# A row softmax on one core: TensorE in place of SyncE waits for the last stores

## The chip, the cores and the metric

The kernel runs on one core of a Trainium2 chip. A core has five engines, each with its own stream of instructions: TensorE (PE), VectorE (DVE), ScalarE (ACT), GpSimd (POOL) and SyncE (SP). They meet only through semaphores, counters that one instruction raises and another waits for. Transfers between the chip's main memory (HBM) and the core's working memory are made by 16 DMA engines; here SP alone issues them. The metric is the time of one execution on the device, in microseconds (us).

## The reference

A softmax over the last axis of a float32 array of 16 x 1024 x 512, that is over 16384 rows of 512 numbers:

```python
x_max = np.max(x, axis=-1, keepdims=True)
exp_x = np.exp(x - x_max)
return (exp_x / np.sum(exp_x, axis=-1, keepdims=True)).astype(np.float32)
```

33.55 MB are read and 33.55 MB written.

## The kernel before

**Tiles.** The 16384 rows are cut into 16 groups of 128 partitions x 8 rows (GROUPS, GROUP). The working memory holds a ring of 12 groups (RING), in which everything is done in place. Eight loads (L0 to L7) and eight stores (S0 to S7) of two groups each (LOADS, STORES) move 4096 KB apiece.

**Stages of a group.** DVE takes the negated maximum of each row (`rowmax`, line 145). ACT runs one loop over all groups (`exps`, lines 150 and 151, its work at line 134): per row an exponential with that maximum as its bias, which also leaves the row's sum. DVE inverts the sums (line 159), and DVE or POOL multiplies the group by them (line 161). Then SP stores it (line 131).

**What sets the order.** All is written out by hand. SEQUENCE is the order of DVE's and POOL's work: M and MM are maxima of one and of two groups, D a scaling on DVE, P one on POOL. ORDER is the order of SP's transfers after the first six loads: S0 S1 L6 L7 S2 S3 S4 S5 S6 S7. The loop at the end of the kernel goes through it; `store_scaled` (lines 169 to 171) waits until both groups of a store are scaled, and a load into a part of the ring that is used again waits for the store of what was there (line 197). The first six loads wait for nothing; `loads_at_the_head` puts the very first ahead of the start barrier. Two more barriers over all engines follow the first loads (they stand at line 179, `tc.close`); the profile shows their waits as EVENT_SEMAPHORE.

**The end.** `done_by` (lines 165 to 167) gives each store the semaphore that it raises by 16 when it has landed: `stored0` and `stored1` for S0 and S1, for which L6 and L7 wait, and one common semaphore, `others`, for S2 to S7 (number 120 in the trace). The last two lines of the kernel are the only place that waits for the stores S2 to S7:

```python
    nc.sync.wait_ge(others, 16 * (len(STORES) - 1 - max(awaited)))
    nc.sync.nop()
```

`awaited` is [0, 1], so the wait is for 16 * (8 - 1 - 1) = 96, six stores. The wait and the nop stand in the built program as one EVENT_SEMAPHORE instruction, the last of SP's stream (line 200 in the profile). TensorE does no work in this kernel; its stream has the barriers and nothing else.

Of the kernel before, what the change touches and what calls it, by code (L numbers as in the profile page):

```python
# [20 lines left out]
STORES = [2, 2, 2, 2, 2, 2, 2, 2]  # L21
# [39 lines left out]
def kernel(  # L61
# [5 lines left out]
    nc = tc.nc  # L67
# [15 lines left out]
    def sem(name):  # L83
        return ctx.enter_context(nc.semaphore(name))
# [18 lines left out]
    awaited = sorted(set(before.values()))  # L103
    stored = {k: sem(f"stored{k}") for k in awaited}
    others = sem("others")
# [19 lines left out]
    def load(k):  # L125
        g, n = LOAD_AT[k], LOADS[k]
        return nc.sync.dma_start(out=rows(g, n), in_=in_dram(x_rows, g, n))
# [62 lines left out]
    for transfer in ORDER.split():  # L190
# [3 lines left out]
        else:  # L194
# [1 line left out]
            since = max([a for a in awaited if a < last], default=-1)  # L196
            nc.sync.wait_ge(stored[last], 16 * (last - since))
            load(k).then_inc(loaded[k], 16)
    nc.sync.wait_ge(others, 16 * (len(STORES) - 1 - max(awaited)))
    nc.sync.nop()  # L200


# [28 lines left out]
```

## Time and profile before

| | |
|---|---|
| time, median of 3 runs | 159.92 us (159.79 to 159.99) |
| the profiled execution's own time | 160.08 us |
| its span, first to last instruction of the program | 158.8 us (158.764 in the trace) |
| DMA queue q1, share of 16 engines' span | 98.9%, 67.11 MB in 2304 packets |
| DVE, ACT, POOL busy | 121.8, 92.2, 42.3 us |
| last store issued by SP | 137.84 us after the span's start |
| wait on line 200 ends | 158.75 us after the span's start |

All times in the profile are counted from the span's start. The span holds only the program's own instructions; what the runtime executes ahead of them and after them lies outside. The page gives each engine's busy time, a strip of 40 equal slices of the span with the busy share of each in tenths, the DMA queues, and a chain that is followed back from the end. A "q" after an engine's name means its sequencer, which waits, branches and issues while the engine itself is idle. Beside instructions, the trace keeps the time of every update of every semaphore.

### The profile page before, as it was taken

How to read it: one execution, taken by the hardware profiler on the slowest of the kernel's cores; microseconds unless marked ns; L12 is line 12 of the kernel's file. 1: busy time of each engine (PE TensorE's matmuls, PEld its weight loads, DVE VectorE, ACT ScalarE, POOL GpSimd, SP SyncE). 2: the span in 40 equal slices, each digit the busy share in tenths (PEclk: the TensorE clock that was granted, in tenths of full speed). 3: DMA queues.
4: the chain of work that ended last, by engine and by line, in shares of the span. 5: the costliest groups of instructions: out<-in, count | busy, mean ns of one | idle time of the engine just before them, and what ended most of it. 6: DMA issues, size and time to landing. Idle time of an engine off the chain costs nothing.

```text
span 158.8 us, 572 instructions
## 1 busy us (share of the span) xinstructions
DVE 121.8 (77%) x36; ACT 92.2 (58%) x257; POOL 42.3 (27%) x10
## 2 busy tenths in 40 slices
DVE  0008979999999999999999499999999999700000
ACT  0300699969406999999988990899599300000000
POOL 0000000000007903930970790079049300000000
DMA  7999999999999999999999999999999999999996
GB/s 264 438 479 405 405 495 421 396 438 471 413 405 438 471 405 396 396 413 471 438 396 462 446 413 405 454 421 438 438 421 446 413 446 438 438 421 438 429 429 264
DMA packets 2304, 67.11 MB, mean 423 GB/s; under 512 B 256, under 2 KB 256, under 8 KB 256
## 3 DMA queue, kind: packets, MB, share of 16 engines
q1 hardware_dynamic: 2304, 67.11, 98.9%
HBM read 33.55 MB, written 33.55 MB: 423 GB/s over the span
## 4 chain that ended last, share of the span: by engine, by line
DMA 45%; DVE 39%; issue 2%; DVEq 0%
DMA ring<-in_x_dram 26%; DVE ring L161 22%; DMA out_dram<-ring 20%; DVE stat L145 16%; DVE recip L159 1%; DVEq L144 0%
## 5 line engine op out<-in xcount | busy, mean ns | idle before, releaser
L134 ACT ACTIVATE ring<-ring,stat x128 | 90.4, 707 | 28.1 <-ACTq L151 28.1
L145 DVE TENSOR_REDUCE stat<-ring 128x16 f32<-128x8192 f32 (+1 forms) x10 | 69.5, 6956 | 15.7 <-DMA ring<-in_x_dram 15.7
L161 POOL TENSOR_TENSOR ring<-ring,recip 128x4096 f32<-128x4096 f32 x6 | 42.1, 7016 | 81.8 <-DVE recip L159 81.8
L161 DVE TENSOR_TENSOR ring<-ring,recip 128x4096 f32<-128x4096 f32 x10 | 51.1, 5109 | 0.3
L134 ACT ACTIVATION_READ_ACCUMULATOR ring<-ring,stat x128 | 23.8, 186 | 0.0
L181 ACT ACT_TABLE_LOAD x1 | 1.3, 1283 | 4.0 <-PEq L179 4.0
L159 DVE RECIPROCAL recip<-stat 128x8 f32<-128x8 f32 x16 | 3.0, 190 | 0.0
L215 POOL MEMSET const-float32-0.0<- 128x1 f32 x1 | 0.1, 98 | 0.2 <-issue 0.2
L215 POOL MEMSET const-bfloat16-1.0<- 128x1 bf16 x1 | 0.1, 102 | 0.0
L215 POOL MEMSET const-uint8-127<- 128x1 uint8 x1 | 0.1, 102 | 0.0
L215 POOL MEMSET const-float32-1.0<- 128x1 f32 x1 | 0.1, 98 | 0.0
## 6 DMA issues: line engine op xcount, KB each, us to landing
ring<-in_x_dram SPq DMA_DIRECT2D x8, 4096.0 KB, 25.9
out_dram<-ring SPq DMA_DIRECT2D x8, 4096.0 KB, 24.0
```

Source lines behind the costliest of these rows:

```text
L134: return nc.scalar.activation(out=row, in_=row, func=EXP, bias=one, scale=1.0, accum_out=one)
L145: nc.vector.reduce_max(out=cols(stat, g, groups), in_=rows(g, groups), axis=AX, negate=True).then_inc(maxima, groups)
L159: nc.vector.reciprocal(out=cols(recip, g), in_=cols(stat, g)).then_inc(inverted, 1)
L161: engine.tensor_mul(out=rows(g), in0=rows(g), in1=spread(cols(recip, g))).then_inc(scaled[store_of(g)], 1)
L181: nc.scalar.preload_act_table(EXP)
L215: nc = _bacc.Bacc("TRN2", target_bir_lowering=False, num_devices=1)
```

## The change

The wait for `others` and the nop behind it are taken from SP's stream and put at the end of TensorE's. The condition, 96, is the same. Every other instruction keeps its engine and its place.

```diff
@@ -196,8 +196,8 @@
             since = max([a for a in awaited if a < last], default=-1)
             nc.sync.wait_ge(stored[last], 16 * (last - since))
             load(k).then_inc(loaded[k], 16)
-    nc.sync.wait_ge(others, 16 * (len(STORES) - 1 - max(awaited)))
-    nc.sync.nop()
+    nc.tensor.wait_ge(others, 16 * (len(STORES) - 1 - max(awaited)))
+    nc.tensor.nop()
```

## The prediction

> **What bounds the kernel now.** I read the page first, for the balance of engines and transfers.
>
> ```profile
> span 158.8 us, 572 instructions
> DVE 121.8 (77%) x36; ACT 92.2 (58%) x257; POOL 42.3 (27%) x10
> ...
> DVE  0008979999999999999999499999999999700000
> ...
> DMA  7999999999999999999999999999999999999996
> ...
> q1 hardware_dynamic: 2304, 67.11, 98.9%
> ...
> DMA 45%; DVE 39%; issue 2%; DVEq 0%
> ```
>
> The DMA row is full from end to end while the busiest engine is at 77%: the transfers set the time. PE has no row: it computes nothing. The chain's shares (DMA 45%, DVE 39%) follow one thread through work that lies under transfers, so I don't take DVE for the bound.
>
> Next SP's waits, the timeline of the end, and the table by stretches, whose last row starts where DVE is done (columns: stretch, its length, busy us of DVE, ACT, POOL, then PE clock, DMA share, GB/s).
>
> ```profile
> SPq L131 <- DVE ring L161: 112.0, 7, 36.0
> SPq L200 <- DMA out_dram<-ring: 20.6, 1, 20.6
> ```
>
> ```profile
> 133.38 4.42 DVE L161 TENSOR_TENSOR ring<-ring,recip 128x4096 f32<-128x4096 f32 x1
> 137.84 0.33 SPq L131 DMA_DIRECT2D out_dram<-ring  x1
> ```
>
> ```profile
> 138.00:159.00 21.00, 0.00 (x0) 0.00 (x0) 0.00 (x0) 1.00 0.92 396
> ```
>
> From 138.2 us on, nothing runs but the stores; SP waits 20.6 us for them on line 200, the wait that the change moves. Then the details of that line and of the barriers of line 179, the only place where PE and SP run the same instruction (ns, minimum/median/maximum; PEld is PE's own sequencer here).
>
> ```profile
> L200 SPq EVENT_SEMAPHORE  x1: 17/17/17, 158.7 to 158.7; - x1
> ```
>
> ```profile
> L179 SPq EVENT_SEMAPHORE  x2: 17/17/17, 3.6 to 3.9; - x2
> L179 ACTq EVENT_SEMAPHORE  x2: 17/17/17, 3.6 to 3.9; - x2
> L179 DVEq EVENT_SEMAPHORE  x2: 21/21/21, 3.6 to 3.9; - x2
> L179 PEldq EVENT_SEMAPHORE  x2: 51/51/51, 3.6 to 3.9; - x2
> ```
>
> One released wait costs PE 51 ns where SP, ACT and POOL need 17.
>
> **What lies after the span.** The profiled execution took 160.08 us, its span 158.764, so 1.32 us are outside. The trace keeps the time of every semaphore's updates, also of those that the program doesn't use. Semaphore 2 is such a one (the program has 96, 97 and 99 to 120), and it is updated nine times in each of several groups, us from the span's start:
>
> ```
> just before the program:  -0.375 -0.341 -0.302 -0.258 -0.235 | -0.123 -0.085 -0.051 -0.004
> closing, first group:      4.184 124.456 124.914 137.959 158.890 | 158.934 158.972 159.007 159.055
> closing, second group:    159.842 159.876 159.914 159.958 159.982 | 160.080 160.118 160.152 160.199
> ```
>
> Between the closing groups nearly all 256 semaphores are updated once, as in a reset: 207 to 255 at 159.015-159.102, 156 to 206 until 159.394, 105 to 155 until 159.422, 54 to 104 until 159.392, 3 to 53 until 159.617. I read this as a relay over the five engines, five steps up and four back, each waiting for the one before. The first closing group names them. At 4.184 us only PE has no work left, so **PE is first**. ACT's last instruction ends at 124.343 and POOL's at 124.386: steps two and three. DVE's ends at 137.808: step four. SP's wait ends at 158.764: step five, **SP is last**. So today everybody has handed on long before, and after the last landing the relay has only SP's step and the way back to do.
>
> **The change, part by part.** It adds no instruction: one wait with its nop, a single EVENT_SEMAPHORE in the trace, leaves SP and stands on PE. The order on each engine is otherwise the same; no DMA is moved, and SP issues all sixteen transfers as before (the last at 137.84). Behind the wait on PE stands only PE's relay step, and **all four other engines wait for that one**.
>
> 1. *Stores and compute: 0.* They don't know who waits. The last update of semaphore 120 (`others`) stays at 158.730.
> 2. *The last engine's arrival.* SP today: update at 158.730, wait starts 158.747 (+17 ns), lasts 17, relay step 126 ns later at 158.890; 160 ns in all. PE on the same road, from its own rows: in the barriers of line 179 PE starts 11 to 12 ns after SP on the same release (3.571 against 3.559, 3.898 against 3.887), so 28; the wait takes 51; from its last wait's end (3.898+0.051 = 3.949) to its relay step at 4.184 it took 235 ns, and from the last reset (159.617) to its next step (159.842) 225. That makes 28+51+235 = 314 ns. **Difference +0.154.** No row shows PE waiting for a DMA's semaphore with the relay behind it. The bounds for the road from the wait's end: 104 ns (ACT, from its last update at 124.352 to 124.456) and at least 528 (the step at 124.914 after POOL's end at 124.386; 571 if it is ACT's). By them the term goes from +0.023 to +0.447. I take 235, since it is PE's own, seen twice.
> 3. *The relay.* Today 158.890 to 159.055: 165 ns. With PE last to come, the whole relay runs after it. Whole relays with all engines waiting are shown: 357 ns (159.842 to 160.199) and 371 (-0.375 to -0.004). **Difference +0.192 to +0.206**, four hops up (34, 38, 44, 24 = 140) and a turn of 98 to 112 in place of 44. Bounds: 0, if the steps up don't depend on the order, and 0.206.
> 4. *Reset and second relay: 0 of their own.* They start from the first relay's end and move as a block. Already PE ends the resets last (159.617) and starts the second relay.
>
> SP's old road of 160 ns goes; it is hidden under the stores, and what is late next is PE's. The sum: 0.154 + 0.20 = **+0.35 us**, 160.43 against the profiled 160.08. That execution is 0.16 above the median of the runs shown (159.92); I carry the difference over: 159.92 + 0.35 = **160.27 us**.
>
> [...] The rows 51 and 17 for the same instruction don't look like equal sequencers, and I follow them. [...]
>
> **The rivals.**
>
> - *PE is no slower in this place* (waiting 155 us, it may have its next steps ready; 235 ns was just after a barrier), or the hops up are not serial. For it: no row shows this situation. Against: 225 ns again in another place, where PE had only resets behind it. Time: +0.20 (or +0.15 if only the relay is missing), 160.07 to 160.12.
> - *Not slower: arrivals are counted in any order, and the engine that comes last leaves first.* Then PE's late arrival (154 ns) is paid back where the way back, 165 ns today, no longer stands before PE's reset, the last to end. Price 0.154 - 0.165 = -0.01, 159.91; it decides as soon as the way back is worth more than PE's lateness. For it: the first closing group alone would look the same. Against: in the second group SP, free at 159.102, doesn't step until PE, free at 159.617, has; and the same gaps of 34, 38-39, 44, 23-24 come back. That is a fixed order.
> - *The time ends with the wait.* Then only the wait's own shift counts: 11 + 34 ns, +0.05, 159.97. Against: 1.32 us lie outside the span, and semaphore 2 goes on for 1.435 us after it, about as long. No view shows where the clock stops.
> - *PE leaves late*, as the step at 124.914 did: 528 in place of 235, +0.64, 160.56. For it: PE would not have run for 155 us. Against: its 235 and 225 agree.
>
> **How the numbers follow.** Forecast +0.35 (own range +0.30 to +0.40, 160.22 to 160.32): 0.72. PE not slower, or no serial hops: 0.12. Any order: 0.06. Ends with the wait: 0.04. Late exit: 0.06. About 0.2%, 0.32 us, is what a measurement of this kernel can tell from no change, and the forecast lies just over it: of its 0.72 I give 0.54 to slower by more and 0.18 to within. Slower: 0.54 + 0.06 = 0.60. Faster 0.02, the scatter of the second and third rival (the three runs lie 0.20 apart). The rest, 0.38, is within. The range goes from the third rival less some scatter, 159.95, to above the forecast with the scatter and half of the late exit, 160.45; it leaves out most of "any order" and of "late exit".
>
> **What would show it.** In the profile after: line 200 on PE with 51 ns, its start some 11 ns further from the last update of 120; SP's last record at 138.2; the span longer by about 0.05 only, since the relay lies outside. In semaphore 2: no updates between the program's start and 159 us, then PE's about 314 ns after the last landing, 34, 38, 44, 24 behind it, a turn near 100, and about 0.67 us from landing to the group's end in place of 0.325. The forecast is wrong in step 2 if that first number is nearer 160 ns, in step 3 if steps of other engines come before PE's, in step 1 if the last landing itself moves.

## The result, and the profile after

| | before | after |
|---|---|---|
| time, median of 7 runs each | 159.92 us (159.79 to 159.99) | 160.44 us (160.23 to 160.61) |
| ratio, 95% interval | | 1.003 [1.002, 1.004] |
| the profiled execution: time, span | 160.08, 158.764 us | 160.61, 158.994 us |
| last landing: the last raise of `others` (120) by a store, from the span's start | 158.730 us | 158.914 us |
| time of that execution less this landing | 1.350 us | 1.696 us |

Slower by 0.52 us, of the sign forecast; the sum had said +0.35. The measured 160.44 lies outside the forecast's own range (160.22 to 160.32) and only 0.01 us under the end of the whole range, 160.45. That end had been set for scatter and for half of a late exit of PE; the exit did not come, so that the time still lies inside is in part luck. The last row of the table holds the forecast sum: after the last store has landed, the changed kernel needs **0.346 us** more. The rest lies ahead of the landing and is taken up below.

The page of after; the lines answer to those shown of before:

```profile
span 159.0 us, 572 instructions
DVE 121.8 (77%) x36; ACT 92.3 (58%) x257; POOL 42.3 (27%) x10
...
DMA  7999999999999999999999999999999999999996
...
q1 hardware_dynamic: 2304, 67.11, 98.9%
...
DMA 45%; DVE 39%; issue 2%; DVEq 0%
```

Little in it tells of a change: 572 instructions again, busy times within 0.1 us, the same queue share and chain. The span alone is longer, by 0.230 us: 0.184 of it lies ahead of the landing, 0.046 is the wait's own shift (80 ns from the landing to the wait's end in place of 34). A page of the program's own span can't show a cost that is paid after it. SP's waits and the details of line 200 show what moved (ns, minimum/median/maximum, then first and last start in us):

```profile
SPq L131 <- DVE ring L161: 111.9, 7, 35.8
SPq L127 <- DMA out_dram<-ring: 18.9, 2, 9.5
```

```profile
L200 PEldq EVENT_SEMAPHORE  x1: 51/51/51, 158.9 to 158.9; - x1
```

SP's wait of 20.6 us is gone from its list; the same wait is now PE's, and lasts 51 ns after its release in place of 17. The rest is in semaphore 2 (us from the span's start):

```
closing, first group:     159.229 159.263 159.301 159.345 159.369 | 159.466 159.506 159.540 159.587
closing, second group:    160.378 160.412 160.450 160.494 160.518 | 160.616 160.654 160.689 160.735
```

Before, four of the five steps up stood at 4.184, 124.456, 124.914 and 137.959 us, long before the last landing. Now all nine come after it, PE's first, 315 ns behind the landing, and the whole first group runs 34, 38, 44, 24, 97, 40, 34 and 47 ns from step to step. It ends 673 ns after the landing; before it was 325.

### The profile page after: what moved, and what is told of

Same layout as the page of the kernel before. It is cut to its first block, busy times and chain, and to the rows that moved or that the text cites. A ratio compares the mean times of both kernels' runs of the same rounds, so it can differ in the third digit from the quotient of the medians.

```text
span 159.0 us, 572 instructions
## 1 busy us (share of the span) xinstructions
DVE 121.8 (77%) x36; ACT 92.3 (58%) x257; POOL 42.3 (27%) x10
## 4 chain that ended last, share of the span: by engine, by line
DMA 45%; DVE 39%; issue 2%; DVEq 0%
DMA ring<-in_x_dram 25%; DVE ring L161 22%; DMA out_dram<-ring 20%; DVE stat L145 16%; DVE recip L159 1%; DVEq L144 0%
## 5 line engine op out<-in xcount | busy, mean ns | idle before, releaser
L134 ACT ACTIVATION_READ_ACCUMULATOR ring<-ring,stat x128 | 24.4, 190 | 0.0
```

What stands on the lines that cost most here:

```text
L134: return nc.scalar.activation(out=row, in_=row, func=EXP, bias=one, scale=1.0, accum_out=one)
```

## The experiments

My theory: the five engines leave the program through a relay in the fixed order PE, ACT, POOL, DVE, SP and back; the engine that comes last pays its own road to its step (the time from the end of its wait to its update of semaphore 2), and all that stands behind its place runs after it. Rivals: only the last comer's road counts, not its place; an engine that stays inside the program, or an SP that is free under the stores, makes the transfers longer, which would be the missing 0.17 us. Since the landing scatters by some tenths from execution to execution (158.307 to 158.914 us), I read each run by what follows its own landing. All rows are from one profiled execution each:

| who waits for the stores | landing to that engine's step, ns | landing to the first group's end, ns | time less landing, us |
|---|---|---|---|
| SP (before; built anew) | 160; 160 | 325; 325 | 1.350; 1.352 |
| PE (after; second; third time) | 315; 314; 314 | 673; 672; 672 | 1.696; 1.697; 1.700 |
| SP and PE | 314 (PE's) | 672 | 1.694 |
| SP, PE until the last scaling | 160 | 322 | 1.349 |
| DVE | 193 | 435 | 1.456 |
| ACT | 157 | 480 | 1.503 |
| POOL | 578 | 864 | 1.888 |
| SP, and four more waits | 410 | 575 | 1.598 |
| PE, and four more waits | 742 | 1099 | 2.123 |

In all twelve profiles the last column is the one before it plus 1.021 to 1.028 us: what follows the first group costs the same whoever waits.

Time and span are also known for every single run, the span to 0.1 us, so the part outside the span can be averaged over all runs, without semaphore 2. The kernel before has 1.312, 1.318 and 1.328 us (35, 25 and 17 runs, by chip), built anew 1.313 (12). The changed kernel has 1.627 in its seven first runs and 1.618 and 1.623 in the repeats (12 each), with SP waiting too 1.633 (12), with PE's early exit 1.309 (12). The 0.30 us between the two kernels is the 0.346 less the 0.046 that the wait adds inside the span.

### The change again, twice

No edit.

> The changed kernel once more. The relay theory (PE's late arrival plus the whole relay) accounts for 0.348 us of the measured +0.52. If the other 0.17 was scatter of the transfers, the difference to the kernel before is now +0.30 to +0.40 us; if it belongs to the change (transfers land later because SP or PE stands elsewhere), it is again +0.47 to +0.57. In the profile either way 315 ns from the last landing to PE's relay step, and 673 ns to the end of the relay.

Measured: 160.29 us against 159.92 for the kernel before on the same chip, ratio 1.0021 [1.0007, 1.0034]: +0.37.

> The changed kernel a third time, for the size alone. Relay theory: +0.35 us, within 0.08. If the first measurement's +0.52 was right, +0.5 or more.

Measured: 160.23 against 159.84, ratio 1.0027 [1.0015, 1.0039]: +0.39. Both medians agree with +0.35 and lie under +0.52, though their intervals still reach it. The last landings of these two profiles are 158.603 and 158.390 us, earlier than the 158.730 of before; in the first profile of the change it was 158.914.

### SP and PE both wait

```diff
     nc.sync.wait_ge(others, 16 * (len(STORES) - 1 - max(awaited)))
     nc.sync.nop()
+    nc.tensor.wait_ge(others, 16 * (len(STORES) - 1 - max(awaited)))
+    nc.tensor.nop()
```

> SP and PE both wait for the stores. Relay theory: the same as PE alone, +0.35 us, since PE is still the last to reach its first place in the relay; SP, at its step after 160 ns, waits for the others. Rival, SP that is free from 138 us on disturbs the transfers: here SP isn't free, so +0.35 where the changed kernel has +0.52. Rival, a PE that is still inside the program lengthens the transfers: +0.52 here too.

Measured: 160.21 us, ratio 1.0016 [1.0006, 1.0025]: +0.29; after the landing exactly PE's 314 and 672 ns. The two waits on one semaphore, first SP's (line 200), then PE's (line 202), in two answers of the trace:

```profile
L200 SPq EVENT_SEMAPHORE  x1: 17/17/17, 158.4 to 158.4; - x1
```

```profile
L202 PEldq EVENT_SEMAPHORE  x1: 51/51/51, 158.4 to 158.4; - x1
```

SP starts at 158.422, PE at 158.434, 12 ns later, as the barriers of line 179 had shown; SP's earlier end doesn't help, since it is fifth in line. A free SP is not what makes the change slow. Nor does a PE inside the program lengthen the transfers by anything seen here: the landing, 158.406, is among the earliest of all, and the mean span of the 12 runs is 158.59 us against 158.65 for the kernel before.

### PE leaves before the stores end

```diff
+    nc.tensor.wait_ge(scaled[7], STORES[7])
+    nc.tensor.nop()
     nc.sync.wait_ge(others, 16 * (len(STORES) - 1 - max(awaited)))
     nc.sync.nop()
```

> SP waits for the stores as before; PE waits until the last group is scaled (137.8 us). Relay theory: 0.00 us (within 0.05), PE's relay step comes near 138.1 us, under the last store. Rival, a PE inside the program lengthens the transfers: up to +0.15. Rival, the relay needs PE's step early: +0.2 or more.

Measured: 159.97 against 159.92, ratio 0.9999 [0.9987, 1.0011]. PE's wait ends at 137.80 us, under the last store:

```profile
L200 PEldq EVENT_SEMAPHORE  x1: 51/51/51, 137.8 to 137.8; - x1
```

and semaphore 2 shows the order of the relay most plainly:

```
closing, first group:     138.037 138.071 138.109 138.153 158.801 | 158.844 158.883 158.917 158.963
```

ACT and POOL were done at 124.235 and 124.290, but their steps come at 138.071 and 138.109, 34 and 38 ns behind PE's. So the steps up are serial and begin with PE. PE's 235 ns (137.802 to 138.037) are there again and cost nothing, because the last store covers them: it leaves more than 20 us until SP's step.

### The kernel before, built anew

No edit.

> The kernel before itself, built anew: every theory says 0.00 us. It shows how far the last landing scatters from run to run and from build to build; if it is off by 0.1 us or more, the 0.17 us that the relay doesn't account for is inside that scatter.

Measured: 159.90 against 159.92, ratio 0.9996 [0.9985, 1.0007]. Its 12 runs reach from 159.69 to 160.24, the 35 of the kernel before beside it from 159.71 to 160.67. The scatter of single runs is larger than the effect; medians of some ten runs and the part after the landing are what it can be read from.

### ACT, DVE or POOL waits

Each puts the two lines on another engine, here ACT; `nc.vector` and `nc.gpsimd` in the other two:

```diff
-    nc.sync.wait_ge(others, 16 * (len(STORES) - 1 - max(awaited)))
-    nc.sync.nop()
+    nc.scalar.wait_ge(others, 16 * (len(STORES) - 1 - max(awaited)))
+    nc.scalar.nop()
```

> ACT waits for the stores in place of SP. Relay theory, from the last landing to the end of the first closing relay: 21 ns to the wait's start, 17 for the wait, 104 to 113 for ACT's road to its step, then POOL 38, DVE 44, SP 24, turn 98, POOL 38, ACT 34, PE 47: 465 to 474 ns against 325 with SP, so +0.14 to +0.15 us. Rival, only the last comer's own road counts and not its place: 142 to 151 against SP's 160, so -0.01 us. Rival, any late engine other than SP costs the same as PE: +0.35.

> DVE waits for the stores in place of SP. Relay theory: 27 ns to the wait's start, 21 for the wait, 151 for DVE's road, then SP 24, turn 98, POOL 38, ACT 34, PE 47: 440 ns against 325, so +0.115 us. Rival, only the own road counts: 199 against 160, +0.04. Rival, the same as PE: +0.35.

> POOL waits for the stores in place of SP. Relay theory: some 17 ns to the wait's start, 17 for the wait, then POOL's road, which is open: 153 ns by its road from the relay to the resets, 528 by its step at 124.914 in the trace of the kernel before. After it DVE 44, SP 24, turn 98, POOL 38, ACT 34, PE 47 = 285: 472 ns and +0.15 us by the short road, 847 ns and +0.52 by the long one. Rival, only the own road counts: +0.03 or +0.40.

Measured, after the landing: ACT 480 ns (expected 465 to 474), DVE 435 (440), POOL 864 (847 by the long road); in the time of the profiled execution less its landing +0.153, +0.106 and +0.538 us against before. The medians can't decide for ACT and DVE: 160.01 and 159.99 against 159.96, ratios 0.9999 [0.9983, 1.0016] and 1.0007 [0.9990, 1.0025], which allow no change as well as the expected sums; POOL has 160.41, ratio 1.0037 [1.0020, 1.0054]. The part outside the span, averaged over the ten runs each, does decide: 1.463, 1.410 and 1.849 us against 1.318, that is +0.145, +0.092 and +0.531. The first groups and the waits of ACT and DVE:

```
ACT waits:   4.200 158.464 158.502 158.546 158.569 | 158.667 158.707 158.741 158.787
DVE waits:   4.151 124.432 124.889 158.657 158.681 | 158.778 158.818 158.852 158.899
POOL waits:  4.177 124.303 159.110 159.154 159.177 | 159.275 159.315 159.349 159.396
```

```profile
L200 ACTq EVENT_SEMAPHORE  x1: 17/17/17, 158.3 to 158.3; - x1
```

```profile
L200 DVEq EVENT_SEMAPHORE  x1: 21/21/21, 158.5 to 158.5; - x1
```

ACT decides against "only the road counts": it gets to its step in 157 ns, faster than SP's 160, and still the relay ends 155 ns later, because POOL, DVE, SP and the whole way back stand behind it. POOL's wait is as short as SP's:

```profile
L200 POOLq EVENT_SEMAPHORE  x1: 17/17/17, 158.6 to 158.6; - x1
```

but from its end (158.574) to POOL's step (159.110) it takes 536 ns, so the long interval of the kernel before, 528, was POOL's own. So the place alone does not decide either: POOL is third, PE first, and POOL costs more, by its road.

### Four more waits on PE, and on SP

```diff
     nc.tensor.wait_ge(others, 16 * (len(STORES) - 1 - max(awaited)))
     nc.tensor.nop()
+    for _ in range(8):
+        nc.tensor.wait_ge(others, 16 * (len(STORES) - 1 - max(awaited)))
+        nc.tensor.nop()
```

The eight waits are built into four instructions with two conditions each. The same on SP, added to the kernel before, with `nc.sync`. Both are from a single execution each (161.01 and 160.35 us), so they are read by what follows their own landing alone.

> PE waits as in the changed kernel and then four times more, for what is already fulfilled. If PE's 235 ns to its relay step is made of several instructions that PE's sequencer takes slowly, each more wait costs between 51 ns (its own length) and 151 ns (from one wait's start to the next instruction in the barriers): 0.20 to 0.60 us more than the changed kernel, from landing to PE's step 0.52 to 0.92. If only the release from a wait is slow on PE, four waits that need no release cost next to nothing: below 0.1 us.

> SP waits as in the kernel before and then four times more, for what is already fulfilled; the counterpart of the run with four more on PE, where each cost 107 ns. If PE's sequencer takes every such instruction about three times as slowly as SP's (51 against 17 ns in the rows), each more wait costs SP 35 to 45 ns and the time from landing to SP's step goes from 160 to 300-340 ns. If the two sequencers are equal and PE is slow elsewhere, it costs SP 107 ns each too, about 590 ns in all.

The waits on PE (two lines of code, as pairs of conditions fall):

```profile
L203 PEldq EVENT_SEMAPHORE  x3: 51/51/51, 158.9 to 159.4; - x3
L202 PEldq EVENT_SEMAPHORE  x2: 51/51/51, 159.0 to 159.3; - x2
```

and on SP:

```profile
L202 SPq EVENT_SEMAPHORE  x2: 28/28/28, 158.8 to 159.0; - x2
L203 SPq EVENT_SEMAPHORE  x3: 17/28/28, 158.8 to 159.0; - x3
```

On PE the step came 742 - 315 = 427 ns later, 107 for each wait; on SP 410 - 160 = 250, 63 each, where I had expected 35 to 45. These steps include the road, which is a little shorter here: 189 ns in place of 235 on PE, 114 in place of 126 on SP. By the starts alone the waits follow each other at 118 ns on PE (111, 150, 106, 106) and at 63 on SP (64, 67, 59, 62). So PE is slower at each of these waits and not only at a release, but 1.7 to 1.9 times, not 3. That would fit a road of several instructions (235 against 126 ns, 1.9 times); the trace has none of the road's instructions, so this much is my reading, not shown.

## Why the prediction was right, point by point

- **Step 1, stores and compute, 0:** right in the repeats, and the term that was off in the first measurement; by the prediction's own sign ("if the last landing itself moves") it failed there. Between the two profiled executions, 0.53 us apart, the landing moved from 158.730 to 158.914, +0.184, which is what they have over +0.346. The seven first runs show the same: outside the span they have 1.627 us, as the repeats, but their mean span is 158.80 us against 158.72 and 158.66. Nothing ties this to the change: over the twelve profiles the landing lies anywhere between 158.307 and 158.914, and the spans of the repeats are 0.06 and 0.12 us above those of the kernel before on the same chip, that of "SP and PE" 0.06 below, where the wait's shift is 0.046. The forecast's own range left too little for this scatter. Why six of the seven first runs came out above the repeats' medians stays open; I call it scatter because it didn't come back, and found no cause for it.
- **Step 2, the last engine's arrival, 314 against 160 ns:** measured 315, 314, 314; in the first of them 29 to the wait's start, 51 for the wait and 235 for the road, where the sum had 28, 51 and 235. PE's own two rows, 235 and 225, were the right ones to take; the bound of 528 belonged to POOL. (The barriers of line 179 are not, as the prediction says, the only place where PE and SP run the same instruction: the start barrier, line 215, has it too, with the same 51 and 17 ns.)
- **Step 3, the relay, 357 to 371 in place of 165 ns:** measured 358 (159.229 to 159.587). The run with PE's early exit shows the order that the prediction had inferred.
- **Step 4, reset and second relay move as a block:** right. From the first group's end to the second's it is 1144 ns before and 1148 after.
- **The rivals.** PE no slower: out, 314 ns. Any order: out, ACT and POOL waited 14 us for PE's step. Ends with the wait: out, the time less the landing grew by 0.346, not by 0.045. PE leaves late: out for PE, true of POOL.

None of the five engines beats SP, and the order of the relay says why: SP is fifth, so only the way back, 165 ns, is left when it comes. No version tried is faster than the kernel before; the one with PE's early exit equals it.

## What to carry to other kernels

In this program the last wait belongs on the engine whose place in the closing relay is last and whose road to it is short: SP here, then DVE (+0.106 us), ACT (+0.153), PE (+0.346), POOL (+0.538). The order of these five was measured here alone, on one core and under one runtime; whether another program has the same order is not shown. An engine without work was not free of cost as the place for this wait (PE, +0.346 us); ask what stands behind it once the wait is over. When the span's views show no difference, look at what follows the span: the updates of a semaphore that the program doesn't use gave this sum to a few ns, far finer than the medians.

## What the runs showed of the hardware that was not expected

- POOL took 528 to 536 ns from its last instruction in the program to its step in the relay, where SP took 126 to 128, ACT 113 to 118, DVE 144 to 153 and PE 234 to 235 (after four more waits, SP 114 and PE 189). What it does in that time is not in the trace.
- In all twelve profiles the execution's own time, counted from the span's start, falls on the sixth step of the second closing group, within 6 ns (160.08 and 160.080 before, 160.61 and 160.616 after). That the clock stops there is only read off; it may as well start some 0.12 us late and stop at the ninth step.
- A wait for two conditions that were both fulfilled lasted 28 ns on SP, one for a single condition 17; on PE both lasted 51.
